# Stick-breaking attention: the later blocks' sum enters through a block's latest key, and two tokens of each block are swapped

## The chip, the cores and the metric

The kernel runs on one core of one Trainium2 chip. A core has a matrix engine (TensorE, PE in the profile; PEld is its loading of weights), VectorE (DVE), ScalarE (ACT), GpSimd (POOL) and SyncE (SP), which here issues the DMAs. The metric is the device time of one execution in microseconds, lower is better.

## The reference

The program is an encoder trunk of two layers over 1024 tokens of width 1024, each layer a mixer and a SwiGLU. The change is in layer 0's mixer, which has 8 heads of stick-breaking attention beside 8 heads of latent attention:

```
before = s_pos < t_pos
log_keep = jnp.where(before, jax.nn.log_sigmoid(-z), 0.0)
log_between = lax.cumsum(log_keep, axis=3, reverse=True) - log_keep
w_b = jnp.where(before, jnp.exp(jax.nn.log_sigmoid(z) + log_between), 0.0)
```

For a query t, each key s before it gets the weight of its own score times what all keys between s and t leave over. So the sum of `log_keep` runs over the keys from the latest one down to s, across all blocks of keys.

## The kernel before, in words

Keys stand in the 128 partitions, queries in the free dimension, two heads at a time (a pair, `p` = 0 to 3). A pass over one half of the queries (`hf`, 512 columns) goes through the blocks of 128 keys from the latest to the earliest, 4 blocks for the first half and 8 for the second, 48 block steps in all. Where a key block lies in the half itself (a diagonal step) only the later columns are worked on, 128, 256, 384 or 512 wide; the other steps have the full 512.

`sb_step` writes a block step as three stages. `scores` makes the scores z in a pair of PSUM banks (L894, L895), clips them into SBUF (L897, VectorE), takes exp and ln of 1 + exp (L898, L899, ScalarE), takes the larger of that and the score (L900, VectorE), clears the entries above the diagonal with a select on POOL (L888), and splits the result t into a rounded part sh (L904, ScalarE) and a rest sl (through the helper's line L248: head 0 on VectorE, head 1 on POOL). `weights` sums over keys with matrix products: a triangular matrix of ones, `tri`, times sh (L916) and times sl (L921), and for all blocks but the first a matrix of ones times `carry` (L919). The carry is a tile whose rows 0 and 32 hold the rounded part (L923, ScalarE) and the rest (L924, VectorE) of the row 0 of the sum, which is the sum over all keys so far. Then come the subtraction z minus sum (L927), exp (L928) and for diagonal steps the select again. `outputs` multiplies the weights with the values, one head per product (L831).

`step` keeps the stages of several blocks in flight. With LAG = 2, a block's `weights` are written two steps after its `scores`, and its `outputs` two after that. Between the steps `weave` puts filling work, projections for the next pair (L280 to L282) or, in pair 3, the preparation of the latent attention; `cost` and `total` set how much. A scheduler then orders the instructions of each engine, except in the feed-forward parts, which are pinned. An engine runs its instructions in that order. Tile tags bound how far ahead things may go: two pairs of score banks (`z`), three tiles `b` (t and the carry), four tiles `c` (sh and sl).

Of the kernel before, what the change touches and what calls it, by code (L numbers as in the profile page):

```python
# [22 lines left out]

GROUPS = [3, 3, 3, 2]
NEG = -(2.0 ** 100)
ZMAX = 88.0
MM_US = 0.216
HEAP = 60
# [2 lines left out]
LAG = 2  # L31
# [125 lines left out]
class Trunk:  # L157
# [47 lines left out]
    def load_consts(self):  # L205
        nc, a, cp = self.nc, self.a, self.cp
        self.g = cp.tile([P, G_N], F32, name="gains")
        nc.sync.dma_start(self.g, a["gains"])
# [8 lines left out]
        nc.gpsimd.affine_select(out=raw[:, 0:P], in_=self.ones, pattern=[[-1, P]], compare_op=ALU.is_ge,  # L217
                                fill=0.0, base=0, channel_multiplier=1)
        nc.vector.memset(raw[:, P:2 * P], 1.0)
        nc.vector.memset(raw[:, 2 * P:], 0.0)  # L220
        self.masks = cp.tile([P, HALF], F32R, name="masks")
        nc.vector.tensor_copy(self.masks, raw)
        self.tri, self.carry_ones = self.masks[:, 0:P], self.masks[:, P:2 * P]
        self.zeros = self.masks[:, 2 * P:3 * P]
# [650 lines left out]
    def sb_step(self, p, hf, j, proj, vt, st, o_d):  # L875
        nc = self.nc
        mm = nc.tensor.matmul
# [4 lines left out]
        top = j == 4 * hf + 3  # L882
        c0 = r * P if diag else 0
        cs = slice(c0, HALF)
        x = {}

        def causal(t):
            nc.gpsimd.affine_select(out=t, in_=t, pattern=[[0, 2], [1, P]], compare_op=ALU.is_gt,  # L888
                                    fill=0.0, base=0, channel_multiplier=-1)

        def scores():
            z = self.banks()
# [7 lines left out]
            nc.vector.tensor_tensor(t[:, :, cs], t[:, :, cs], zc[:, :, cs], ALU.max)  # L900
# [3 lines left out]
            nc.scalar.copy(sh[:, :, cs], t[:, :, cs])  # L904
            for e in range(2):
                self.rest(("dve", "pool")[e], sl[:, e, cs], t[:, e, cs], sh[:, e, cs])
            x.update(zc=zc, sh=sh, sl=sl)

        def weights():
            if top:  # L910
                st["carry"] = self.tmp("b", F32R)
                nc.gpsimd.memset(st["carry"].bitcast(F32), 0.0)
            carry = st["carry"]
            b = self.banks()
            for e in range(2):
                mm(b[:, e, cs], self.tri, x["sh"][:, e, cs], start=True, stop=False)  # L916
            if not top:
                for e in range(2):
                    mm(b[:, e, cs], self.carry_ones, carry[:, e, cs], start=False, stop=False)  # L919
            for e in range(2):  # L920
                mm(b[:, e, cs], self.tri, x["sl"][:, e, cs], start=False, stop=True)  # L921
            if j > 0:
                nc.scalar.copy(carry[0:1, :, cs], b[0:1, :, cs])  # L923
                nc.vector.tensor_tensor(carry[32:33, :, cs], b[0:1, :, cs], carry[0:1, :, cs].bitcast(F32),  # L924
                                        ALU.subtract)
            w = x["zc"]
            nc.vector.tensor_tensor(w[:, :, cs], w[:, :, cs], b[:, :, cs], ALU.subtract)  # L927
            nc.scalar.activation(w[:, :, cs], w[:, :, cs], AF.Exp)  # L928
            if diag:
                causal(w[:, :, c0:c0 + P])  # L930
# [469 lines left out]
    return np.stack([_ktiles(w, np.arange(i, i + m)) for i in range(0, w.shape[1], m)])  # L1400


def _layout(i):
    out = {}
    xT = np.ascontiguousarray(i["x"][0].T)
# [46 lines left out]
    s = np.arange(P)[:, None]  # L1452
    x = np.arange(640)[None, :]
    out["bias_k"] = np.ascontiguousarray(rb[:, np.clip(x - s, -256, 256) + 256])
    out["bias_q"] = np.ascontiguousarray(rb[:, np.clip(512 + s - x, -256, 256) + 256])
    pos = np.arange(S, dtype=np.float32)
# [32 lines left out]
```

## Time and profile before

| what | us |
|---|---|
| median of three runs (lowest, highest) | 2609.49 (2604.78, 2610.32) |
| the profiled execution's own time | 2615.43 |
| its span, first to last instruction | 2613.3 |
| PE busy in the span | 2521.6 |
| VectorE busy | 1911.5 |
| ScalarE busy | 1169.0 |
| POOL busy | 522.9 |

Busy time of a matrix product includes its way through the array; products follow each other at less than their own duration. A row of a group gives line, engine, operation, output<-input by name, shape and count, then busy us and the mean ns of one, then the idle us of the engine just before them and what ended it. A row in order of time gives start and duration in us.

### The profile page before, as it was taken

The numbers are of one execution on the slowest core, as the hardware profiler recorded it, in microseconds if no ns is written. First come the engines' busy times: TensorE is split into PE (matmuls) and PEld (weight loads), VectorE is DVE, ScalarE is ACT, GpSimd is POOL, SyncE is SP. The second block draws the span as 40 slices with busy tenths as digits, with TensorE's granted clock in tenths as the row PEclk, the third lists the DMA queues.
The fourth block names the chain that finished last, engine by engine and source line by source line (L and its number), as shares of the span: only waits on it lengthen the run. The fifth ranks groups of instructions, "written<-read, shape, count | busy, mean of one in ns | idle before, by whom it ended". The sixth has DMA issues, their size and how long they took to land.

```text
span 2613.3 us, 33627 instructions
## 1 busy us (share of the span) xinstructions
PE 2521.6 (96%) x11758; PEld 1941.0 (74%) x11758; DVE 1911.5 (73%) x3072; ACT 1169.0 (45%) x2028; POOL 522.9 (20%) x489
## 2 busy tenths in 40 slices
PE   7999999999999999999999999999999999999997
PEld 6766765557778888888787666676777888888876
DVE  6888887775787666777666777777778766667776
ACT  4677676454454334432253333334444443443324
POOL 3333324663000000000021333335400000000004
PEclk9999998999999999999999999999999999999999
DMA  4221100125434344476642222222552434447661
GB/s 137 61 63 53 53 17 29 35 64 159 163 99 161 110 140 142 149 258 216 206 160 67 73 78 80 73 69 89 172 166 96 162 109 141 145 140 260 213 213 69
DMA packets 179433, 319.70 MB, mean 122 GB/s; under 512 B 20545, under 2 KB 36801, under 8 KB 179265
## 3 DMA queue, kind: packets, MB, share of 16 engines
q1 hardware_dynamic: 179264, 317.56, 36.8%
q8 instruction: 93, 1.52, 0.3%
q14 instruction: 76, 0.61, 0.1%
HBM read 222.58 MB, written 84.41 MB: 117 GB/s over the span
## 4 chain that ended last, share of the span: by engine, by line
PE 68%; DVE 12%; DMA 2%; issue 2%; ACT 2%; SPq 0%; DVEq 0%; ACTq 0%
PE z L74 24%; PE mm L74 12%; PE o L74 6%; PE mm L280 5%; PE mm L281 5%; PE mm L282 5%; PE o L831 3%; DVE u L74 2%; DVE f L1093 2%; PE z L1201 1%; PE z L1175 1%; PE z L1202 1%; DVE u L303 1%; DMA wr<-in_w_down 1%; PE z L1088 1%
## 5 line engine op out<-in xcount | busy, mean ns | idle before, releaser
L74 PE MATMUL z<-u,vh 128*128 128x512 f32 x976 | 304.6, 393 | 7.2 <-DVE u L74 7.2
L74 PE MATMUL z<-u,wh 128*128 128x512 f32 x976 | 302.3, 390 | 6.5 <-DVE u L74 6.5
L280 PE MATMUL mm<-u,wh 128*128 128x512 f32 x720 | 291.7, 405 | 2.4 <-DVE u L710 1.1
L281 PE MATMUL mm<-u,wh 128*128 128x512 f32 x720 | 284.4, 395 | 1.4 <-DVE u L248 1.4
L248 POOL TENSOR_TENSOR wl<-wr,wh 128x512 fp32r<-128x512 f32 (+2 forms) x95 | 123.6, 1308 | 802.4 <-ACT wh L243 733.6
L282 PE MATMUL mm<-u,wl 128*128 128x512 f32 x720 | 283.8, 394 | 0.0
L74 PE MATMUL mm<-u,wh 128*128 128x512 f32 x720 | 224.6, 393 | 3.8 <-ACT wh L74 3.8
L74 PEld LDWEIGHTS z<-u,vh 128*128 128x128 f32 x976 | 184.5, 189 | 48.1 <-ACT u L74 8.8
L74 PEld LDWEIGHTS z<-u,wh 128*128 128x128 f32 x976 | 183.1, 188 | 47.4 <-DVE u L74 9.4
L74 PE MATMUL z<-u,vl 128*128 128x512 f32 x488 | 191.1, 392 | 0.0
L74 PE MATMUL z<-u,wl 128*128 128x512 f32 x488 | 190.0, 389 | 0.0
L280 PEld LDWEIGHTS mm<-u,wh 128*128 128x128 f32 x720 | 135.6, 188 | 62.2 <-issue 33.1
L831 PE MATMUL o<-a,u 128*64 128x512 f32 (+3 forms) x768 | 172.4, 485 | 0.3 <-ACT a L1204 0.3
L74 PEld LDWEIGHTS mm<-u,wh 128*128 128x128 f32 x720 | 135.5, 189 | 34.9 <-ACT wh L74 5.7
L281 PEld LDWEIGHTS mm<-u,wh 128*128 128x128 f32 x720 | 135.8, 189 | 32.5 <-issue 8.3
L282 PEld LDWEIGHTS mm<-u,wl 128*128 128x128 f32 x720 | 135.5, 188 | 32.3 <-issue 3.6
L74 PE MATMUL mm<-u,vh 128*128 128x512 f32 x496 | 152.7, 389 | 0.0
L248 POOL TENSOR_TENSOR u<-wr,u 128x512 fp32r<-128x512 f32 x8 | 10.9, 1373 | 671.7 <-ACT u L243 671.7
L74 PE MATMUL mm<-u,wl 128*128 128x512 f32 x360 | 141.2, 392 | 0.7 <-DVE wl L74 0.5
L1204 ACT ACTIVATE a<-a 128x1024 f32<-128x1024 f32 (+3 forms) x96 | 70.6, 738 | 155.3 <-DVE a L1203 155.0
L1072 POOL TENSOR_TENSOR b<-b,a 128x512 f32<-128x512 f32 (+3 forms) x80 | 110.6, 1382 | 135.8 <-ACT a L1204 117.4
L1203 DVE TENSOR_TENSOR a<-z,bias 128x1024 f32<-128x1024 f32 (+3 forms) x96 | 78.7, 823 | 79.5 <-PE z L1202 65.6
(248 smaller groups left out, 5983.1 us busy)
## 6 DMA issues: line engine op xcount, KB each, us to landing
u<-f_t SPq DMA_DIRECT2D x144, 256.0 KB, 5.2
vr<-in_w_up SPq DMA_DIRECT2D x88, 256.0 KB, 4.4
wr<-in_w_gate SPq DMA_DIRECT2D x88, 256.0 KB, 3.5
f_t<-x SPq DMA_DIRECT2D x72, 256.0 KB, 2.0
wr<-in_w_out SPq DMA_DIRECT2D x64, 256.0 KB, 3.0
f_t<-e SPq DMA_DIRECT2D x54, 256.0 KB, 3.6
ld<-f SPq DMA_DIRECT2D x54, 256.0 KB, 5.2
h<-u SPq DMA_DIRECT2D x48, 256.0 KB, 2.5
```

The lines of the kernel that those rows point to most:

```text
L74: return lambda *a, **k: self.tc.keep_in_program_order(f(*a, **k))
L248: self.eng(eng).tensor_tensor(lo, src, hi.bitcast(F32), ALU.subtract)
L280: mm(out, wh, xh, start=first, stop=False, skip_group_check=onto)
L281: mm(out, wh, xl, start=False, stop=False, skip_group_check=onto)
L282: mm(out, wl, xh, start=False, stop=last, skip_group_check=onto)
L303: self.eng(eng).tensor_tensor(acc, acc, sq, ALU.add)
L831: self.nc.tensor.matmul(o[rh, cs], vt[j // 4][:, j % 4, rh], w[:, e, cs], start=first, stop=last)
L1072: self.eng("dve" if dest[2] else "pool").tensor_tensor(st["esum"][:, :, cs], old[:, :, cs], ex[:, :, cs], ALU.add)
L1088: nc.tensor.matmul(den[64 * e:64 * e + 64, :], self.ones[:, 0:64], esum[:, e, :], start=True, stop=True)
L1093: nc.vector.scalar_tensor_tensor(r, t, 2.0, r, ALU.add, ALU.mult)
L1203: nc.vector.tensor_tensor(ex[:, :, cs], z[:, :, cs], tk[:, :, xs], ALU.add)
L1204: nc.scalar.activation(ex[:, :, cs], ex[:, :, cs], AF.Exp)
```

## The change

The rows of `order` shown here use names with a serial number (z_1225 is a pair of banks, here the sum of one block; b_ is t, c_ is sh or sl, a_ the clipped score and later the weight, mm_ and wh_ / wl_ belong to filling projections, o_ is the output).

A block step gets a stage `parts` between `scores` and `weights`. It adds row 0 of the later block's sum, from PSUM, to one row of t, and only then splits t into sh and sl. Since `tri` sums from the latest key down, a value added at the block's latest key reaches all keys of the block, and row 0 of the new sum again holds everything so far. The products with the matrix of ones, the carry tile with its cast, its subtraction and its clearing are gone.

[...] The triangular order is no longer that of the partitions; a 128 x 128 matrix `before` is loaded, `tri` is ones minus that matrix, and the two diagonal masks are multiplications with it on POOL instead of selects. Lines of the changed kernel: minimum L898, exp and ln L899 and L900, maximum L901, mask L890, row addition L910, cast L912, rests L250, sums L921, subtraction L924, exp L925, outputs L833.

```
 def causal(t):
-    nc.gpsimd.affine_select(out=t, in_=t, pattern=[[0, 2], [1, P]], compare_op=ALU.is_gt,
-                            fill=0.0, base=0, channel_multiplier=-1)
+    nc.gpsimd.tensor_tensor(t, t, self.before[:, None, :].to_broadcast([P, 2, P]), ALU.mult)
...
+    x.update(zc=zc, t=t)
+
+def parts():
+    t = x["t"]
+    if not top:
+        above, c1 = st["sum"]
+        nc.vector.tensor_tensor(t[LATEST:LATEST + 1, :, c1:], t[LATEST:LATEST + 1, :, c1:], above[0:1, :, c1:], ALU.add)
     sh, sl = self.tmp("c", F32R), self.tmp("c", F32R)
     nc.scalar.copy(sh[:, :, cs], t[:, :, cs])
...
 def weights():
-    if top:
-        st["carry"] = self.tmp("b", F32R)
-        nc.gpsimd.memset(st["carry"].bitcast(F32), 0.0)
-    carry = st["carry"]
     b = self.banks()
-    for e in range(2):
-        mm(b[:, e, cs], self.tri, x["sh"][:, e, cs], start=True, stop=False)
-    if not top:
+    for part in ("sh", "sl"):
         for e in range(2):
-            mm(b[:, e, cs], self.carry_ones, carry[:, e, cs], start=False, stop=False)
-    for e in range(2):
-        mm(b[:, e, cs], self.tri, x["sl"][:, e, cs], start=False, stop=True)
-    if j > 0:
-        nc.scalar.copy(carry[0:1, :, cs], b[0:1, :, cs])
-        nc.vector.tensor_tensor(carry[32:33, :, cs], b[0:1, :, cs], carry[0:1, :, cs].bitcast(F32),
-                                ALU.subtract)
+            mm(b[:, e, cs], self.tri, x[part][:, e, cs], start=part == "sh", stop=part == "sl")
+    st["sum"] = b, c0
...
-idle = [lambda: None] * (LAG - 1)
-self.step(scores, *idle, weights, *idle, outputs)
+idle = lambda: None
+self.step(scores, parts, weights, idle, outputs)
...
+order = np.arange(P)
+order[[LATEST, P - 1]] = order[[P - 1, LATEST]]
...
+self.before = cp.tile([P, P], F32, name="before")
+nc.sync.dma_start(self.before, a["before"])
 raw = self.tmp("f")
...
+nc.vector.tensor_tensor(raw[:, 0:P], self.ones, self.before, ALU.subtract)
+nc.vector.memset(raw[:, P:], 0.0)
```

The order on VectorE in the full-width steps of pair 0, second half. Before (L924 makes the carry's rest from the sum z_1252, L927 is the subtraction of the same sum):

```order
L924 TENSOR_TENSOR b_999<-z_1252,b_999 1x1024
L248 TENSOR_TENSOR c_1177<-b_1171,c_1176 128x512
L927 TENSOR_TENSOR a_1125<-a_1125,z_1252 128x1024
L897 TENSOR_SCALAR a_1268<-z_1263 128x1024
L897 TENSOR_SCALAR a_1334<-z_1329 128x1024
L924 TENSOR_TENSOR b_999<-z_1318,b_999 1x1024
L900 TENSOR_TENSOR b_1269<-b_1269,a_1268 128x1024
L927 TENSOR_TENSOR a_1170<-a_1170,z_1318 128x1024
```

The same place in the changed kernel (L924 is now the subtraction, L910 the row addition of the same sum; L250 to c_ is the rest of head 0):

```order
L924 TENSOR_TENSOR a_1106<-a_1106,z_1225 128x1024
L901 TENSOR_TENSOR b_1149<-b_1149,a_1148 128x1024
L898 TENSOR_SCALAR a_1243<-z_1238 128x1024
L910 TENSOR_TENSOR b_1149<-b_1149,z_1225 1x1024
L247 CAST wh_1381<-wr_1379 128x512
L250 TENSOR_TENSOR wl_1382<-wr_1379,wh_1381 128x512
L250 TENSOR_TENSOR c_1234<-b_1149,c_1233 128x512
L901 TENSOR_TENSOR b_1244<-b_1244,a_1243 128x1024
L924 TENSOR_TENSOR a_1148<-a_1148,z_1288 128x1024
L910 TENSOR_TENSOR b_1244<-b_1244,z_1288 1x1024
```

Where the row for the carry stood ahead of the subtraction and the rest c_ did not need it, the subtraction now stands first, the row addition behind it, and the rest c_1234 behind the row addition of z_1225.

The order on PE in the same steps. Before (one block's sum z_1387 in a row: tri times sh, ones times carry, tri times sl):

```order
L831 MATMUL o_1104<-a_1125,u_526 64x512 x2
L916 MATMUL z_1387<-c_1274,masks 128x512 x2
L919 MATMUL z_1387<-b_999,masks 128x512 x2
L921 MATMUL z_1387<-c_1275,masks 128x512 x2
L894 MATMUL z_1398<-u_873,u_1082 128x128
L895 MATMUL z_1398<-u_873,u_1084 128x128
```

In the changed kernel (z_1354 is the sum of the same block):

```order
L283 MATMUL mm_1391<-u_207,wh_1381 128x512
L284 MATMUL mm_1391<-u_206,wl_1382 128x512
L833 MATMUL o_1083<-a_1148,u_527 64x512
L921 MATMUL z_1354<-c_1296,masks 128x512 x2
L921 MATMUL z_1354<-c_1297,masks 128x512 x2
L895 MATMUL z_1367<-u_863,u_1061 128x128
L896 MATMUL z_1367<-u_863,u_1063 128x128
L895 MATMUL z_1367<-u_864,u_1062 128x128
L896 MATMUL z_1367<-u_864,u_1064 128x128
L833 MATMUL o_1083<-a_1148,u_527 64x512
```

The products with the carry are gone from the sum, and the two heads of one output (o_1083<-a_1148) stand on both sides of it.

More of the change, by code (lines that the diff above doesn't have):

```diff
@@ L25 @@
 NEG = -(2.0 ** 100)
+LATEST = 96
 ZMAX = 88.0
@@ L215, in load_consts @@
                                 fill=0.0, base=0, channel_multiplier=-1)
+        self.before = cp.tile([P, P], F32, name="before")
+        nc.sync.dma_start(self.before, a["before"])
         raw = self.tmp("f")
[L217 to L220, printed above, removed]
+        nc.vector.tensor_tensor(raw[:, 0:P], self.ones, self.before, ALU.subtract)
+        nc.vector.memset(raw[:, P:], 0.0)
         self.masks = cp.tile([P, HALF], F32R, name="masks")
         nc.vector.tensor_copy(self.masks, raw)
-        self.tri, self.carry_ones = self.masks[:, 0:P], self.masks[:, P:2 * P]
-        self.zeros = self.masks[:, 2 * P:3 * P]
+        self.tri, self.zeros = self.masks[:, 0:P], self.masks[:, P:2 * P]
         self.negblk = cp.tile([4, 4], F32, name="negblk")
@@ L906, in scores @@
                 self.rest(("dve", "pool")[e], sl[:, e, cs], t[:, e, cs], sh[:, e, cs])
[L907 removed]
+            x.update(sh=sh, sl=sl)
         def weights():
[L910 to L913 removed]
             b = self.banks()
[L915 to L917 removed]
+            for part in ("sh", "sl"):
                 for e in range(2):
[L919 to L925 removed]
+                    mm(b[:, e, cs], self.tri, x[part][:, e, cs], start=part == "sh", stop=part == "sl")
+            st["sum"] = b, c0
             w = x["zc"]
@@ L1400, in _mtiles, with _order @@
     return np.stack([_ktiles(w, np.arange(i, i + m)) for i in range(0, w.shape[1], m)])
+def _order():
+    order = np.arange(P)
+    order[[LATEST, P - 1]] = order[[P - 1, LATEST]]
+    return order
 def _layout(i):
     out = {}
-    xT = np.ascontiguousarray(i["x"][0].T)
+    perm = _order()
+    tokens = (np.arange(0, S, P)[:, None] + perm).reshape(-1)
+    out["before"] = (perm[:, None] < perm[None, :]).astype(np.float32)
+    xT = np.ascontiguousarray(i["x"][0][tokens].T)
     out["x"] = np.ascontiguousarray(xT.reshape(KD, P, 2, HALF).transpose(2, 0, 1, 3))
@@ L1451, in _layout @@
     rb = i["od_rel_bias"][0]
-    s = np.arange(P)[:, None]
-    x = np.arange(640)[None, :]
+    s = perm[:, None]
+    x = (np.arange(0, 640, P)[:, None] + perm).reshape(1, -1)
     out["bias_k"] = np.ascontiguousarray(rb[:, np.clip(x - s, -256, 256) + 256])
     out["bias_q"] = np.ascontiguousarray(rb[:, np.clip(512 + s - x, -256, 256) + 256])
-    pos = np.arange(S, dtype=np.float32)
+    pos = tokens.astype(np.float32)
     inv = (np.float32(10000.0) ** (-np.arange(0, 32, 2, dtype=np.float32) / np.float32(32))).astype(np.float32)
@@ L1487 @@
     y = r.results[0]["out_y"]
-    return np.ascontiguousarray(y.transpose(0, 3, 1, 2).reshape(1, S, D))
+    y = y.transpose(0, 3, 1, 2).reshape(S // P, P, D)
+    return np.ascontiguousarray(y[:, np.argsort(_order())].reshape(1, S, D))
```

## The prediction

> **What bounds the kernel now.** I read the page first, then the stages of the stick-breaking part, then the groups by line and shape, then single rows in order of time.
>
> ```profile
> span 2613.3 us, 33627 instructions
> PE 2521.6 (96%) x11758; PEld 1941.0 (74%) x11758; DVE 1911.5 (73%) x3072; ACT 1169.0 (45%) x2028; POOL 522.9 (20%) x489
> ```
>
> TensorE (PE) is busy for 96% of the span, so a product taken away is worth its time wherever PE stays the bound. The part that changes runs from about 60 to 420 us. Busy time per stage there, columns PE, PEld, DVE, ACT, POOL, granted clock:
>
> ```profile
> 109.00:147.00 38.00, 36.73 (x196) 26.57 (x195) 34.76 (x39) 27.75 (x38) 11.38 (x11) 1.00 0.15 41
> 183.00:220.00 37.00, 35.94 (x192) 26.25 (x192) 34.64 (x38) 26.43 (x36) 10.31 (x11) 1.00 0.16 47
> 256.00:294.00 38.00, 36.88 (x156) 24.96 (x155) 37.15 (x41) 26.88 (x32) 13.19 (x12) 1.00 0.21 57
> 360.00:400.00 40.00, 33.17 (x122) 20.96 (x120) 39.38 (x49) 27.64 (x43) 13.61 (x10) 0.87 0.05 15
> ```
>
> The first three rows are the full-width steps of pairs 0, 1 and 2: PE is the bound there, but VectorE (DVE) stands at 91, 94 and 98%. The last row lies in pair 3: VectorE has no pause and PE is idle for 6.8 of 40 us, so there VectorE sets the time.
>
> **What is removed.** 80 products of the carry with the ones matrix (L919), 40 casts (L923), 40 one-row subtractions (L924) and 8 clearings.
>
> ```profile
> L919 PE MATMUL z<-b,masks x80: 274/393/496, 82.0 to 416.2; 128*128 128x512 f32 x48, 128*128 128x256 f32 x16, 128*128 128x384 f32 x16
> 182.13 0.39 PE L894 MATMUL z<-u,u 128*128 128x512 f32 x1
> 182.36 0.39 PE L895 MATMUL z<-u,u 128*128 128x512 f32 x1
> 191.07 0.28 PE L281 MATMUL mm<-wl,u 128*128 128x256 f32 x1
> 191.19 0.28 PE L282 MATMUL mm<-wh,u 128*128 128x256 f32 x1
> ```
>
> Products overlap, so their price is the distance of their starts: 0.227 us at 512 columns (0.23 in this pair of rows), 0.12 at 256, by interpolation 0.17 at 384. 48 x 0.227 + 16 x 0.17 + 16 x 0.12 = **15.5 us of PE**. In pair 3 four of these steps lie in the stretch that VectorE sets; 8 x 0.227 = **1.8 us** of it is lost.
>
> ```profile
> L923 ACT CAST b<-z 1x1024 fp32r<-1x1024 f32 (+3 forms) x40 | 29.6, 741 | 13.4 <-PE z L921 13.2
> L924 DVE TENSOR_TENSOR b<-z,b 1x1024 fp32r<-1x1024 f32 x16 | 19.4, 1214 | 3.5 <-ACT b L923 3.0
> L912 POOL MEMSET b<- 128x1024 f32 x8 | 7.7, 957 | 0.0
> ```
>
> ScalarE is relieved of 29.6 us and POOL of 7.7 us; neither engine is a bound (45% and 20% of the span), so both count as nothing. The 40 subtractions are replaced by 40 row additions with the same shapes, one operand in PSUM and one in SBUF as before: VectorE's load stays the same. I take 1.21 us for one at 1024, by L924.
>
> **What is moved: the chain from block to block.** Before, the split into high and low parts didn't need the later block's sum; only L919 did, between the high and the low products. Now it runs: low products end, subtraction (L924 of the changed kernel), row addition, cast, rest on POOL, next low products. Durations:
>
> ```profile
> L927 DVE TENSOR_TENSOR a<-a,z 128x1024 f32<-128x1024 f32 x24 | 29.2, 1216 | 2.4 <-PE z L921 2.2
> L897 DVE TENSOR_SCALAR a<-z 128x1024 f32<-128x1024 f32 x24 | 29.2, 1216 | 5.0 <-PE z L895 4.8
> L904 ACT CAST c<-b 128x1024 fp32r<-128x1024 f32 x24 | 25.0, 1043 | 7.6 <-POOL b L888 6.5 <-DVE b L900 1.1
> 194.30 1.30 POOL L248 TENSOR_TENSOR c<-b,c 128x512 fp32r<-128x512 f32 x1 [5.77 <-issue]
> 196.07 1.21 DVE L900 TENSOR_TENSOR b<-b,a 128x1024 f32<-128x1024 f32 x1
> 127.79 1.08 PE L831 MATMUL o<-a,u 128*64 128x512 f32 x4
> 140.71 1.07 PE L831 MATMUL o<-a,u 128*64 128x512 f32 x2
> 141.71 0.50 PE L282 MATMUL mm<-u,wl 128*128 128x512 f32 x1
> ```
>
> Where the addition stands right behind the subtraction, the low part is ready 1.22 + 1.21 + 1.04 + 1.30 + 0.2 for the hops = 5.0 us after the low products before it. Where the order has a maximum and a minimum between them (z_1225 in the rows shown), 2.4 us more: 7.4 us. Against that stands PE's work between the two, counted from the order. From z_1225 to z_1288: 47 products of 256 and 2 of 512 columns, 6.05 us, then the high products and three score products, 1.14: PE arrives at 7.2 us and waits about 0.3. From z_1288 to z_1354: 1 + 6 of 512, 11 of 256, an output pair at 1.0, a lone head's output at 1.0, high products 0.45: 5.35 us against 5.0, no wait. The same sum for the 30 passages of pairs 0 to 2 leaves ten of them short, by 0.03 to 1.56 us, **4.0 us** together. If VectorE comes to each subtraction late by 0.25 us, it is 7.5 us; by 0.5, 12.2; by 1.0, 24.4. Queued behind a late addition are the next minimum and the weights' rests, so what is late next is a score bank and the filling products. Walking VectorE's rows through z_1225 to z_1354 at the durations above I find it 0.1 to 0.25 us late, so I take **7.5 us**; ends for the range: 4.0 and 24.4.
>
> The waits before the low products that exist now belong to the old order, and the 7.5 us stand in their place:
>
> ```profile
> L921 PE MATMUL z<-c,masks 128*128 128x512 f32 x48 | 16.2, 412 | 2.0 <-DVE c L248 1.3 <-POOL c L248 0.7
> L921 PE MATMUL z<-c,masks 128*128 128x384 f32 x16 | 4.2, 342 | 0.8 <-DVE c L248 0.8
> L921 PE MATMUL z<-c,masks 128*128 128x128 f32 x16 | 3.6, 277 | 1.3 <-POOL c L248 1.3
> ```
>
> 2.0 + 0.8 + 1.3 = **4.1 us** come back.
>
> **What the new order costs elsewhere.** Two heads' outputs side by side take 1.0 us (x4 above), one head alone takes as long (140.71 to 141.71). In the stick-breaking part four head pairs stood apart (512, 512, 384, 512 columns, 1.0 or 0.75 us each), now six do (four of 512, one of 384, one of 256 at 0.5), 5.25 us against 3.75: **+1.5 us**. The new constant is a load between the gains and x:
>
> ```profile
> 0.81 0.39 SPq L208 DMA_DIRECT2D gains<-in_gains  x1
> 1.26 0.42 SPq L187 DMA_DIRECT2D ld<-in_x  x1
> ```
>
> SyncE's issues stand 0.45 us apart, x and all behind it come that much later: **+0.4 us**. The masks' difference and cast lie in VectorE's pause before x arrives. The swapped layout changes no instruction's shape: 0.
>
> **The masks on POOL.** 64 selects become multiplications with a loaded mask, not shown before at this form; the nearest rows are a select, and POOL's two-input rest of the same 256 elements:
>
> ```profile
> L888 POOL TENSOR_SCALAR_AFFINE_SELECT b<-b 128x256 f32<-128x256 f32 x32 | 14.4, 450 | 80.0 <-DVE b L900 74.4 <-PE mm L281 3.1 <-PE z L894 2.1
> 81.28 0.74 POOL L248 TENSOR_TENSOR c<-b,c 128x256 fp32r<-128x256 f32 x1 [0.74 <-ACT c L904]
> 136.77 1.79 POOL L248 TENSOR_TENSOR c<-b,c 128x512 fp32r<-128x512 f32 x1 [9.36 <-ACT c L904]
> 137.33 2.31 DVE L900 TENSOR_TENSOR b<-b,a 128x1024 f32<-128x1024 f32 x1
> ```
>
> Between 0.45 and 0.74 each, I take 0.74 (it too reads two tensors): 64 x 0.3 = 19 us more on an engine that is busy 20% of the time, and the mask is due one step before the addition. I cost it at 0; if its cover is gone, see the second rival. The last two rows show how: a VectorE maximum that met POOL's rest took 2.31 us, not 1.21. The Trainium skill, SBUF — State Buffer, section "SBUF: two separate sides", says why: the two engines share a port pair, whoever starts first holds it for the whole instruction, and VectorE is shut out when both its inputs lie in SBUF. The trace agrees (1.10 us longer). By that rule the row additions, with one input in PSUM, never wait, but maxima and rests do.
>
> **Sum**, against the profiled execution's 2615.4 us: -15.5 + 1.8 - 4.1 + 7.5 + 1.5 + 0.4 = -8.4, so 2607.0. That execution lies 5.9 above the median of the runs shown (2609.5); against the median the forecast is **2601 us**.
>
> **Rivals.**
>
> First, the chain is covered better than I sum: 29.6 us less on ScalarE lets its casts start at once, and VectorE no longer waits for L923. For it: L924 waited 3.0 us for L923 at full width alone. Against it: VectorE's 98%. Then only 4.0 us of waits, and pair 3 keeps its share: -15.5 - 4.1 + 4.0 + 1.9 = -13.7, 2596 us. Chance 0.17.
>
> Second, the mask multiplications hold up VectorE in the diagonal steps (the mechanism of the rows 136.77 and 137.33). Pairs 0 to 2 have 48 of them; if 4 in 10 meet a two-SBUF instruction and hold it 0.74 us, that is 14 us of VectorE, and with half of it reaching PE, 7 us: 2608, no change. Against it: VectorE has pauses in the diagonal stretches. Chance 0.18.
>
> Third, the other side: the chain decides each full-width step. Its place is VectorE's queue ahead of the row addition. At 1.0 us late per passage the waits are 24.4 us: -15.5 + 1.8 - 4.1 + 24.4 + 1.9 = +8.5, 2618. It turns to a loss from about 0.7 us late. For it: VectorE at 91 to 98%, each of its instructions 1.2 us long, so an arrival in the middle of one costs half of that. Against it: while PE waits, VectorE catches up. Chance 0.17.
>
> Fourth, the change doesn't reach the clock at all, because the gain of pairs 0 to 2 runs into the VectorE stretch of pair 3 and waits there: 2609. Against it: VectorE's load before 360 us leaves it room to come earlier too. Chance 0.06.
>
> **How the numbers follow.** Forecast 0.42 (2596 to 2605 in itself), rivals 0.17, 0.18, 0.17, 0.06. A measurement of this kernel can tell about 0.2%, 5.2 us, from no change. Faster: 0.34 of the forecast, the first rival 0.17, 0.01 of the fourth: 0.52. Same: 0.08 of the forecast, 0.15 of the second, 0.01 and 0.03 of the third and fourth: 0.27. Slower: 0.03, 0.16 and 0.02: 0.21. The range 2590 to 2614 takes in the first two rivals and goes halfway into the third.
>
> **What would show it.** Right: no products with the ones matrix; PE busy about 15 us less; waits of L921 for the rests and the casts of 5 to 10 us together; from the first to the last tri product some 8 us less. Wrong: VectorE's maxima above 1.4 us in the mean (second rival); L921 waits above 15 us, with VectorE at 95% or more in the diagonals too (third); PE idle in pair 3 grown by what the earlier pairs gained (fourth).

## The result, and the profile after

| kernel | median us (lowest, highest; runs) | ratio to before, 95% interval |
|---|---|---|
| before | 2608.55 (2604.51, 2610.34; 6) | 1 |
| changed | 2623.30 (2615.97, 2626.08; 6) | 1.0056 [1.0041, 1.0072] |

The change makes the kernel slower by 14.6 us (0.0056 x 2608). The forecast was 2601 us, 8.4 us faster. Its range ended at 2614, so the sign and the range were both wrong. Among the experiments below, one run of e3 took 6586.76 us, far outside its other nine (2605 to 2612), and is left out.

The first two lines of the page of the changed kernel:

```profile
span 2620.6 us, 33417 instructions
...
PE 2511.9 (96%) x11678; PEld 1926.4 (74%) x11678; DVE 1933.0 (74%) x3072; ACT 1141.9 (44%) x1988; POOL 535.6 (20%) x480
```

The 80 products are gone (x11758 to x11678), ScalarE has 27 us less to do, and VectorE has 21.5 us *more*, at the same number of instructions. That growth is the first thing to explain, since the additions have the duration of the subtractions that they replace.

The profiled executions are 2622.66 us after and 2615.43 before, only 7.2 apart. To see where the difference lies I take the first dense product of the feed-forward part, which comes after everything that was changed. These are the views by source line of before and of the changed kernel (durations, then first and last start):

```profile
L74 PEld LDWEIGHTS mm<-u,wh x720: 186/188/331, 659.0 to 2539.1; 128*128 128x128 f32 x180
```

```profile
L76 PEld LDWEIGHTS mm<-u,wh x720: 186/188/329, 669.9 to 2546.5; 128*128 128x128 f32 x180
```

It starts 10.9 us later. From there to the end the profiled execution of before takes 3.6 us longer than that of the changed kernel, in work whose instructions the diff leaves as they were. That execution lies 6.9 us above its median, so the difference of the two profiles understates the loss.

Busy time per stage in the changed kernel, columns PE, PEld, DVE, ACT, POOL, granted clock:

```profile
60.00:160.00 100.00, 94.01 (x470) 67.88 (x471) 88.25 (x109) 56.49 (x89) 35.57 (x39) 1.00 0.22 61
160.00:260.00 100.00, 88.20 (x419) 59.93 (x419) 90.44 (x105) 59.20 (x87) 43.84 (x45) 0.97 0.19 55
260.00:360.00 100.00, 92.72 (x410) 65.42 (x409) 86.69 (x99) 55.95 (x76) 36.46 (x38) 1.00 0.17 48
360.00:440.00 80.00, 69.13 (x262) 44.76 (x260) 69.50 (x86) 53.87 (x99) 27.05 (x22) 0.94 0.07 21
```

and the same stages of before:

```profile
60.00:160.00 100.00, 96.33 (x491) 71.22 (x489) 84.80 (x113) 65.90 (x104) 33.44 (x44) 1.00 0.22 60
160.00:260.00 100.00, 96.31 (x484) 68.88 (x485) 87.59 (x111) 71.09 (x104) 40.17 (x53) 1.00 0.22 61
260.00:360.00 100.00, 98.86 (x445) 71.89 (x445) 82.55 (x104) 65.69 (x91) 32.62 (x39) 1.00 0.15 46
360.00:440.00 80.00, 69.07 (x263) 45.65 (x262) 69.44 (x85) 56.34 (x103) 30.08 (x23) 0.89 0.07 22
```

In pairs 0 to 2 (60 to 360 us) PE is idle for 25.1 us, against 8.5 before. In the last row, pair 3, PE's busy time is the same; the pair itself, from its first score product to its last triangular one, takes 131.4 us against 132.0. From the first triangular product of all to the last the changed kernel takes 351.3 us, 13.3 longer than before. The waits of PE from 40 to 440 us in the changed kernel (total, times, longest) say on what:

```profile
PE z L921 <- DVE c L250: 13.6, 21, 1.2
PE o L833 <- POOL a L890: 8.2, 8, 4.9
...
PE z L921 <- POOL c L250: 2.3, 4, 0.6
PE z L921 <- ACT c L912: 2.1, 4, 0.9
```

Before, the first and the third of these were:

```profile
PE z L921 <- DVE c L248: 2.0, 4, 0.8
PE z L921 <- POOL c L248: 2.0, 4, 1.1
```

So the triangular products wait 18.0 us for what comes out of the new chain, priced at 7.5, and the output products wait 8.2 us for a masked weight, priced at nothing. The groups by line and shape, 60 to 440 us, of the changed kernel (busy us, mean ns, idle before):

```profile
L250 POOL TENSOR_TENSOR c<-b,c 128x512 fp32r<-128x512 f32 x24 | 38.3, 1594 | 67.3 <-ACT c L912 65.2 <-POOL u L859 1.9
L250 DVE TENSOR_TENSOR c<-b,c 128x512 fp32r<-128x512 f32 x24 | 37.7, 1572 | 5.4 <-ACT c L912 4.9
...
L901 DVE TENSOR_TENSOR b<-b,a 128x1024 f32<-128x1024 f32 x24 | 30.7, 1279 | 0.2
...
L890 POOL TENSOR_TENSOR b<-b,before 128x256 f32<-128x256 f32 x32 | 28.4, 889 | 44.1 <-DVE b L901 29.6 <-issue 14.5
...
L910 DVE TENSOR_TENSOR b<-b,z 1x1024 f32<-1x1024 f32 x16 | 19.4, 1215 | 0.5
```

and of the rests and the maxima before:

```profile
L248 POOL TENSOR_TENSOR c<-b,c 128x512 fp32r<-128x512 f32 x24 | 35.3, 1470 | 80.0 <-ACT c L904 62.6 <-issue 17.3
...
L900 DVE TENSOR_TENSOR b<-b,a 128x1024 f32<-128x1024 f32 x24 | 31.5, 1313 | 2.6 <-ACT b L899 2.2
...
L248 DVE TENSOR_TENSOR c<-b,c 128x512 fp32r<-128x512 f32 x24 | 24.5, 1020 | 3.3 <-ACT c L904 3.2
```

The addition costs what was forecast (1215 ns), and the maxima have not grown (1279 ns; 1313 before). VectorE's rest has, from 1020 to 1572 ns: 13.2 us of VectorE's new load is in this one row. One passage shows how (start, duration; the rows are from the views of ScalarE, POOL, VectorE and PE in turn):

```profile
191.75 1.06 ACT L912 CAST c<-b 128x1024 fp32r<-128x1024 f32 x1
...
192.94 1.74 POOL L250 TENSOR_TENSOR c<-b,c 128x512 fp32r<-128x512 f32 x1 [0.41 <-POOL u L859]
...
192.84 0.68 DVE L250 TENSOR_TENSOR u<-u,u 64x512 fp32r<-64x512 f32 x1
193.44 1.79 DVE L250 TENSOR_TENSOR c<-b,c 128x512 fp32r<-128x512 f32 x1
...
195.28 0.74 PE L921 MATMUL z<-c,masks 128*128 128x512 f32 x2 [0.34 <-DVE c L250]
```

Both rests need the one cast, which ends at 192.81. POOL's starts first, since VectorE has another piece of 0.68 us ahead of its own, and VectorE's lasts until 0.55 us after POOL's has ended (195.23 against 194.68). The low products start 2.47 us after the cast; the forecast gave this link 1.30 us and a hop. Over the 19 full-width passages from 60 to 360 us, the mean from the cast's end to the end of the later rest is 2.35 us. It was 1.93 us before already (21 passages), only not on a chain from block to block.

### The profile page after: what moved, and what is told of

It is laid out like the page before. It is cut to its first block, busy times and chain, and to the rows that moved or that the text cites. A ratio compares the mean times of both kernels' runs of the same rounds, so it can differ in the third digit from the quotient of the medians.

```text
span 2620.6 us, 33417 instructions
## 1 busy us (share of the span) xinstructions
PE 2511.9 (96%) x11678; PEld 1926.4 (74%) x11678; DVE 1933.0 (74%) x3072; ACT 1141.9 (44%) x1988; POOL 535.6 (20%) x480
## 4 chain that ended last, share of the span: by engine, by line
PE 72%; DVE 18%; issue 3%; ACT 3%; DMA 3%; POOL 1%; SPq 0%; DVEq 0%; POOLq 0%; ACTq 0%
PE z L76 24%; PE mm L76 12%; PE o L76 6%; PE mm L282 6%; PE mm L283 6%; PE mm L284 6%; PE o L833 4%; DVE u L76 2%; DVE f L1090 2%; PE z L1198 1%; DVE c L250 1%; PE z L1172 1%; DVE wl L250 1%; DVE b L901 1%; PE z L1199 1%
## 5 line engine op out<-in xcount | busy, mean ns | idle before, releaser
L250 POOL TENSOR_TENSOR wl<-wr,wh 128x512 fp32r<-128x512 f32 (+2 forms) x95 | 125.0, 1322 | 792.3 <-ACT wh L245 723.6
L833 PE MATMUL o<-a,u 128*64 128x512 f32 (+3 forms) x768 | 174.8, 486 | 9.3 <-POOL a L890 8.2
L250 POOL TENSOR_TENSOR u<-wr,u 128x512 fp32r<-128x512 f32 x8 | 10.9, 1375 | 669.3 <-ACT u L245 669.3
```

Source lines behind the costliest of these rows:

```text
L250: self.eng(eng).tensor_tensor(lo, src, hi.bitcast(F32), ALU.subtract)
L833: self.nc.tensor.matmul(o[rh, cs], vt[j // 4][:, j % 4, rh], w[:, e, cs], start=first, stop=last)
```

## Experiments

In each run a scheduler orders the instructions anew, so an edit may move a few hundred rows besides its own. Times in us below are (ratio - 1) x 2608, and the uncertainty of a difference of two is worked out from both intervals.

| edit | median us (runs) | ratio, 95% interval | us to before |
|---|---|---|---|
| changed kernel | 2623.30 (6) | 1.0056 [1.0041, 1.0072] | +14.6 |
| e1: before, masks multiplied | 2612.18 (10) | 1.0015 [1.0006, 1.0024] | +3.9 |
| e2: changed, old selects | 2617.60 (8) | 1.0033 [1.0023, 1.0044] | +8.6 |
| e3: changed, sum not handed on | 2609.33 (9) | 1.0004 [0.9994, 1.0014] | +1.0 |
| e5: changed, addition first | 2622.23 (4) | 1.0053 [1.0038, 1.0068] | +13.8 |
| e4: changed, both rests on VectorE | 2612.27 (10) | 1.0014 [1.0005, 1.0024] | +3.7 |
| e6: changed, copy on ScalarE | 2611.59 (10) | 1.0010 [0.9999, 1.0021] | +2.6 |
| e7: before, copy on ScalarE | 2598.93 (8) | 0.9963 [0.9953, 0.9973] | -9.6 |
| e8: e6, addition first | 2600.68 (8) | 0.9972 [0.9961, 0.9982] | -7.3 |
| e9: before, both rests on VectorE | 2601.30 (5) | 0.9968 [0.9956, 0.9981] | -8.3 |
| e11: before, both edits | 2598.16 (5) | 0.9951 [0.9937, 0.9965] | -12.8 |
| e12: changed, both edits | 2595.29 (5) | 0.9948 [0.9935, 0.9960] | -13.6 |
| e10: e12, addition first | 2591.45 (5) | 0.9933 [0.9921, 0.9946] | -17.5 |
| e13: changed, row added to itself | 2615.08 (5) | 1.0034 [1.0021, 1.0046] | +8.9 |
| e14: e13, old selects | 2607.05 (11) | 0.9994 [0.9985, 1.0004] | -1.6 |
| e15: e4, old selects | 2610.34 (11) | 1.0006 [0.9997, 1.0015] | +1.6 |
| e16: e4, addition first | 2615.99 (5) | 1.0035 [1.0022, 1.0047] | +9.1 |
| e17: e13, copy on ScalarE | 2613.44 (12) | 1.0017 [1.0008, 1.0027] | +4.4 |
| e18: e14, copy on ScalarE | 2605.39 (12) | 0.9985 [0.9974, 0.9995] | -3.9 |

My theory at the start was that the chain from block to block is longer than priced (the rests) and that the masks cost something. The rivals were VectorE's fullness, and the masks alone.

### The masks: e1 and e2

```
 e1, in before:
-    nc.gpsimd.affine_select(out=t, in_=t, pattern=[[0, 2], [1, P]], ...)
+    nc.gpsimd.tensor_tensor(t, t, self.before[:, None, :].to_broadcast([P, 2, P]), ALU.mult)
 e2, in the changed kernel: the same the other way round
```

> The kernel before, with the loaded mask and the 64 multiplications on POOL in place of the selects, and nothing else: no swap of tokens, the carry as it was. My theory now is that the change lost in two places, the masks (8.2 us of PE waiting for POOL's masks ahead of the outputs in the changed kernel's profile) and the chain through the row addition (18.0 us of PE waiting ahead of the low products). By it the masks alone make the kernel before 4 to 10 us slower. Rival: the chain alone is the loss and the masks are hidden as predicted; then within 3 us of the kernel before.

> The changed kernel with the old selects in place of the multiplications. Left out: the selects follow the order of the partitions, so the two swapped tokens of each block are masked by their place and not by their time; every other instruction is that of the changed kernel. Theory of two places: 6 to 10 us faster than the changed kernel, so some 5 to 9 us slower than the kernel before. Rival, the chain alone: within 3 us of the changed kernel, 12 to 17 us slower than the kernel before.

The edit of e1 is shown without the lines that load the mask, so its figure includes that load. e2 masks the two swapped tokens of each block of 128 (96 and 127) by their place, not by their order. The multiplications cost 3.9 us (+-2.4) in the kernel before and 6.0 (+-4.9) in the changed kernel, each at the lower edge of what my theory said. The forecast had 0, with the price left to the second rival. But the row in which that rival should have shown itself, the maxima, has not grown. What the masks delay is their own readers. In e2 the waits of PE are:

```profile
PE z L922 <- DVE c L250: 14.1, 24, 1.2
PE o L833 <- POOL a L890: 5.2, 2, 4.6
```

The output products wait twice instead of eight times (the longest 4.6 us, close to the changed kernel's 4.9), and the waits for the rests are untouched. So the masks are one part of the loss, and by these two runs the smaller one.

### The sum that goes into the row: e3, e13

```
 e3:
-    nc.vector.tensor_tensor(t[LATEST:LATEST + 1, :, c1:], t[LATEST:LATEST + 1, :, c1:], above[0:1, :, c1:], ALU.add)
+    nc.vector.tensor_tensor(above[0:1, :, c1:], t[LATEST:LATEST + 1, :, c1:], above[0:1, :, c1:], ALU.add)
 e13:
+    nc.vector.tensor_tensor(t[LATEST:LATEST + 1, :, c1:], t[LATEST:LATEST + 1, :, c1:], t[LATEST:LATEST + 1, :, c1:], ALU.add)
```

> The changed kernel with the row addition written back into the bank that it reads, so that the split no longer waits for it. Left out: the later blocks' sum doesn't reach the block; VectorE does the same number of additions of the same shapes. Theory: 14 to 20 us of waits go, 2603 to 2609 us, about the kernel before or up to 5 us faster, with the masks' 8 us still in it. Rival, VectorE's load or the masks are the loss and not the order of the chain: within 5 us of the changed kernel.

> The changed kernel with the row of the latest key added to itself instead of to the later block's row: the addition stays on VectorE, in its place, but waits for no other block, and holds no bank of the earlier sums (the later blocks' sums are left out of the result). Chain theory (the length from block to block is what cost the changed kernel): the chain is gone altogether, so the gain of the products shows, less the masks' multiplications (some 6 us by the run with the old selects): 2598 to 2605. Rival (VectorE's fullness and the rests that hold each other up cost as much without any chain): 2608 to 2616.

In both the later blocks' sums are left out of the result. In e3 the addition stays on VectorE, reads the later block's sum and writes it back there, so the cast no longer waits for it. In e13 the addition still stands ahead of the cast in its own block, but waits for no other block. Its inputs then both lie in SBUF, where e3 has one in PSUM; it lasts as long in both, 1219 and 1222 ns at full width. e3 is at +1.0, at the upper edge of its range. e13 misses my theory's range (2598 to 2605) and falls into the rival's: without any link between blocks the kernel is still 8.9 us slower than before. The two together cut the loss up:

- from the changed kernel to e13, the link between blocks: 5.7 us (+-5.2), barely resolved;
- from e13 to e3, the addition ahead of the cast *inside* a block: 7.9 us (+-4.2), in spite of 3.5 us of a new wait in e3, for the bank that its addition writes.

So a theory of the chain between blocks alone falls. A block's own way from its scores to its low products has grown by an addition, and this by itself costs about as much.

### The order on VectorE: e5

```
 def parts():
     ... row addition ...
+    st["less"]()          # the subtraction, exp and mask of the block before
 def weights():
     ... sums ...
-    subtraction, exp, mask
+    st["less"] = lambda: less(b)      # for j == 0 at once
```

> The changed kernel with the row addition ahead of the subtraction of the same sum: the subtraction, its exp and its mask are written behind the next block's addition. Same instructions, the chain shorter by one subtraction of 1.21 us in most full-width steps. Theory, the length of the chain decides: 8 to 16 us faster than the changed kernel, so between 6 us faster and 7 us slower than the kernel before. Rival, the two rests that hold each other up on the shared port are all of the loss: the chain is shorter, but its end stays as it is, and most of 18 us stays: at most 4 us faster than the changed kernel.

No gain (13.8 against 14.6), where 8 to 16 us were expected. The subtraction of 1.2 us ahead of the addition is not what decides. The waits only change their names, 19.0 us together (18.0 in the changed kernel), among them a new one for the bank that the late subtraction holds:

```profile
PE z L922 <- DVE c L250: 8.5, 13, 1.6
...
PE z L922 <- DVE a L930: 4.1, 4, 1.8
```

### Rests and VectorE's fullness: e4, e6, e7, e8

```
 e4:
-    self.rest(("dve", "pool")[e], sl[:, e, cs], t[:, e, cs], sh[:, e, cs])
+    self.rest("dve", sl[:, e, cs], t[:, e, cs], sh[:, e, cs])
 e6 (changed kernel), e7 (before), e8 (e5 and e6):
-    nc.vector.tensor_scalar(zc[:, :, cs], z[:, :, cs], ZMAX, None, ALU.min)
+    nc.scalar.copy(zc[:, :, cs], z[:, :, cs])
```

> The changed kernel with both heads' rests on VectorE instead of one on POOL. In the changed kernel the VectorE rest takes 1.57 us at 512 columns (1.02 before): it starts with POOL's and they hold each other up. Port theory (the two rests side by side are the loss): 8 to 12 us faster than the changed kernel, since 0.72 + 0.72 us behind each other end sooner than 1.3 + 0.7. VectorE theory (VectorE bounds the full-width steps): what POOL hands over, some 28 us of work, is about what the held-up rests give back, within 5 us of the changed kernel.

> The changed kernel with the score's way out of PSUM on ScalarE (a copy) instead of VectorE (a minimum with 88). Left out: the clip at 88, which these scores don't reach. It takes 46 us of VectorE and gives some 42 us to ScalarE. The runs so far: without the chain the changed kernel only comes back to the time before, with 11 us less PE work and VectorE at 80 to 93%; with the addition first nothing is won. VectorE theory: the full-width steps are bounded by VectorE, so the products that went freed nothing there; with VectorE relieved 14 us or more go, 2600 to 2609 us. Chain theory (length of the chain decides): the chain isn't shorter by it, so at most 6 us faster than the changed kernel, 2617 or more.

> The same move in the kernel before: the score's copy on ScalarE, the clip left out. VectorE theory, if PE and VectorE bound the kernel before in turn: 0 to 6 us faster, since its PE waits in the stick-breaking part are only some 8 us. Then the difference between the changed kernel and this one, both with the move, is the change without VectorE's bound: the changed one is 3 to 10 us faster. Chain theory: the changed one stays 8 us or more slower than this one.

> Both: the row addition ahead of the subtraction, and the score's copy on ScalarE. VectorE theory: once VectorE is no longer the bound, the shorter chain counts: 3 to 8 us faster than the move alone. Rival: the subtraction put behind holds the next sum's bank (4.1 us of PE waiting for it in the run with the addition first), so within 3 us of the move alone.

e6, e7 and e8, and later e10, e11, e12, e17 and e18, leave out the clip of the score at 88.

e4 brings 10.9 us back (+-4.8), as the theory of the rests expected. A rest on VectorE then takes 738 ns in the mean, so two of them one after the other (1476 ns) are done sooner than the one that had shared the work with POOL (1572 ns). The group of e4:

```profile
L250 DVE TENSOR_TENSOR c<-b,c 128x512 fp32r<-128x512 f32 x48 | 33.6, 738 | 0.3
```

e6 brings 12.0 us back (+-5.0) by another way: VectorE gets 48 instructions less, of 1.2 us each at full width. Its time lies between the ranges of both theories. But the same edit in the kernel before brings 9.6, more than the 0 to 6 expected, so the change costs 12.2 us (+-3.9) also where VectorE has room. VectorE's fullness alone is not the cause either. With room there, the order matters: e8 is 9.9 us (+-4.0) under e6 (3 to 8 were expected), although the same reordering brought nothing in e5.

### The controls, and both cures at once: e9 to e12

```
 e9, e11: e4's edit in before, and in e7;  e12: e4's edit in e6;  e10: e4's edit in e8
```

> The kernel before, with both heads' rests on VectorE. Port theory (GpSimd's rest that starts first stops VectorE's for its whole length, and this costs the changed kernel because there it happens on nearly every step, 19 of 24 full-width ones against 8 of 24 before): here little is stopped, VectorE gains the work of a second rest (24 x 0.68 us less the 0.34 us that each of its own is now held up, some 8 to 13 us in all) and the time is the same or worse, 2608 to 2618. Rival (GpSimd's rests are simply slow, and both rests on VectorE are better anywhere): 2600 or less.

> The kernel before with the score's copy on ScalarE and both rests on VectorE, the counterpart without the change of the run with all three edits. Port theory: VectorE has room here, and few rests are held up, so 2597 to 2601, the same as with the copy alone (2599). Rival (GpSimd's rests are slow anywhere): 2595 or less.

> The changed kernel with the score's copy on ScalarE and both rests on VectorE, the addition where the change put it. Port theory: about 10 us under the same kernel with the rests split (2611.6), 2599 to 2604, since the waits on the rests (17 us in the four pairs there) mostly go. Rival (VectorE's fullness is what the split hurt, already cured by the copy's move): 2608 to 2612, no gain from a second cure.

> The changed kernel with the three relieving edits at once: the score's copy on ScalarE (no clip at 88), the row's addition issued ahead of the earlier block's subtraction, both rests on VectorE. Theory (the block to block chain takes the gain, by the held-up rests and by VectorE's fullness): with all three the PE waits on the rests go under 5 us in the four pairs and the gain of some 10 us of products shows against the kernel before with the same copy (2599): 2588 to 2594. Rival (the addition in a row costs PE something that no relief gives back, or the room gained is used up by VectorE's two rests): 2598 or more.

e9 corrects my theory. I expected no gain from it, since in the kernel before the rests are held up less often. It gains 8.3 us, which is close to what its rival said (2600 or less; 2601.30). So the split of the rests is a poor choice in *both* kernels, and with it undone in both the change still costs 12.0 us (+-4.1).

Only together do the two cures turn the result: e12 is level with e11 (1.2 us lower in the mean of five runs each on the same chip), and with the addition first, e10, the changed kernel is under both, by 3.9 us under e12 and by 5.0 under e11 in the means; its runs lie from 2590.36 to 2594.12, those of e11 from 2592.61 to 2599.47. e10 and e11 are where the theory had them (2588 to 2594, 2597 to 2601); e12 went below its range.

The waits of PE for the low products, 40 to 440 us, tell why one cure isn't enough. With the rests on VectorE alone (e4), VectorE is busy for 264.5 of 300 us, the addition comes late in its queue, and the products wait for the cast behind it. In the two longest waits, 2.3 us each, the cast then starts 0.8 us after the addition's end, behind an activation on ScalarE:

```profile
PE z L921 <- ACT c L912: 6.2, 4, 2.3
...
PE o L833 <- POOL a L890: 4.0, 6, 1.5
PE z L921 <- DVE c L250: 3.2, 6, 1.6
PE o L833 <- ACT a L925: 2.8, 2, 1.9
```

With the copy moved alone (e6) VectorE has room (233.3 of 300 us), but the rests still hold each other up:

```profile
PE z L921 <- DVE c L250: 11.9, 14, 1.0
...
PE z L921 <- POOL c L250: 2.7, 6, 0.6
```

With both (e12) little is left of either:

```profile
PE z L921 <- DVE c L250: 2.5, 3, 1.4
...
PE z L921 <- ACT c L912: 1.0, 1, 1.0
```

The busy times from 60 to 360 us of e4, e6 and e12 (PE, PEld, DVE, ACT, POOL):

```profile
60.00:360.00 300.00, 286.13 (x1331) 206.62 (x1332) 264.46 (x365) 179.37 (x259) 62.80 (x82) 0.97 0.20 55
```

```profile
60.00:360.00 300.00, 284.66 (x1341) 203.03 (x1343) 233.25 (x279) 208.77 (x307) 121.32 (x125) 0.99 0.19 55
```

```profile
60.00:360.00 300.00, 293.27 (x1401) 210.70 (x1400) 244.25 (x341) 218.76 (x320) 69.02 (x83) 1.00 0.20 56
```

PE is idle for 13.9, 15.3 and 6.7 us in them, 25.1 in the changed kernel, 8.5 before.

### What was left: e14 to e18

```
 e14, e15: e2's edit in e13, and in e4;  e16: e4's edit in e5;  e17, e18: e6's edit in e13, and in e14
```

> The same with the diagonal masks by the old select (the two swapped tokens are masked by place). If the masks' multiplications cost about 6 us whatever the chain is: 2592 to 2599, or 6 under the run with the row added to itself. If they cost only as a part of the chain from block to block: within 2 us of that run.

> The changed kernel with both rests on VectorE and the old selects (the two swapped tokens masked by place). The changed kernel with both rests on VectorE is 1.0014 of before, the kernel before with the same is 0.9968: 12 us apart, with 6.8 us of PE's waits for masked weights (o L833) and 9.4 for the rests. If the masks are half of it: 2604 to 2608. If the chain through a full VectorE is nearly all of it: 2609 to 2613.

> The changed kernel with both rests on VectorE and the row's addition issued ahead of the earlier block's subtraction, the score's copy left on VectorE. If what is left of the cost there is the place of the addition in VectorE's queue (the subtraction of 1.2 us ahead of it): 2600 to 2606. If it is VectorE's fullness, whatever the order: 2609 to 2613, as without the reordering (it gained nothing with the rests split).

> The changed kernel with the row of the latest key added to itself (no link from block to block; the later blocks' sums are left out) and the score's copy on ScalarE, which relieves VectorE (no clip at 88). It differs from the changed kernel with that copy (1.0010 of before) by the link between blocks alone, and from the run with the row added to itself (1.0034) by the copy alone. If the link costs its 10 us also where VectorE has room, because the rests hold each other up on it: 2598 to 2603. If without the link VectorE's fullness was what was left, nothing else: 2593 to 2598. If neither (the row's addition itself or the masks cost it): 2606 or more.

> The same with the old selects (the two swapped tokens masked by place). Here products are removed, no link, no masks' multiplications, VectorE relieved: if the sum of the parts is right, the gain of the products shows against the kernel before with the same copy (2599): 2586 to 2592. If the row's addition costs what the products brought: 2597 or more.

e14 and e18 leave out the later sums and mask the swapped tokens by place, e15 only the latter, e17 only the former.

- **Masks.** With POOL also doing a rest, the multiplications cost 10.5 us (e13 to e14, +-4.1; e14 was expected at 2592 to 2599 and is at 2607, since e13 was too high already) and 8.3 (e17 to e18, +-3.8); with the rests on VectorE 2.1 (e4 to e15, +-3.5), not to be told from nothing. So it is probably POOL's two jobs together that make them dear. That isn't quite shown: e13 and e17 have no link, e4 has one, and with the link in both kernels 6.0 and 2.1 can't be told apart. The masks aren't half of what e4 has left.
- **Order.** e16 is 5.5 us (+-4.1) *slower* than e4, outside both its ranges (2600 to 2606, 2609 to 2613). The subtraction that was put back holds its bank for longer: 2.8 us of PE's waits are for that bank, where e4 has none. But one wait of 3.8 us in the preparation of the latent attention (L1036) is new as well, and which of the two decides was not separated.
- **The link.** With the copy on ScalarE, taking the link away brings nothing: e17 is at +4.4, e6 at +2.6 (difference 1.8, +-3.9). Its expected 2598 to 2603 was missed by 10 us; the case of 2606 or more, the addition itself or the masks, is the one that came.
- **Products removed, nothing else in the way.** e18 should have shown the whole gain, 2586 to 2592. It is at -3.9, still 5.7 us (+-3.8) worse than the kernel before with the same copy. With the rests split, an addition ahead of the cast, together with the split's new place one stage later, costs more than the 80 products brought, with no link and no multiplication. Its waits:

```profile
PE z L922 <- DVE c L250: 5.9, 7, 1.3
...
PE z L922 <- POOL c L250: 3.1, 6, 0.6
```

## Why the prediction was wrong

**The step that failed is the sum for the moved chain: "1.22 + 1.21 + 1.04 + 1.30 + 0.2 for the hops = 5.0 us".** Its first three terms hold: 1215 ns for the subtraction, 1215 for the addition, 1.05 us for the cast; so do the hops, 0.24 us from addition to cast in the mean of 30 passages of pairs 0 to 2. The rest was mis-sized: it was taken from one row of POOL's rest alone (1.30), with VectorE's beside it. It is 2.35 us until both rests are there, 1.0 us more. The prediction even had a price for a passage that is late by 1.0 us: 24.4 us of waits, and a time of 2618. Measured were 18.0 us of waits, where its list has some 0.7 us of lateness and a time of about 2612. So the lateness that it put in, 0.25 us, was wrong, because lateness was looked for in VectorE's queue *ahead* of the addition only; and the list alone doesn't reach the measured 2623. The rows that showed the step stood in the prediction: a rest of POOL of 1.79 us, and a maximum of 2.31 us that had met it. They were used for the masks and not for the rests, though the mean of POOL's rest was 1470 ns before already. (A slip beside it changes nothing: 7.4 us against 7.2 leaves a wait of 0.2, not 0.3.)

**The chain was drawn between blocks only.** The runs put 7.9 us on the addition ahead of the cast within a block (e13 to e3) and 5.7 on the link, the latter barely resolved and gone when VectorE has room (e17). The prediction compared the chain with the PE work from one block's low products to the next one's. A block's own way from its maximum to its low products, which became longer by the addition, was not summed at all.

**"I cost it at 0"** for the masks: 3.9 to 10.5 us with POOL's rests beside them, 2.1 without. POOL's 20% is a mean over the span. In 60 to 360 us it is 116 of 300, and its instructions there stand close together, a rest that is held up next to a mask. As an estimate, the two terms, 18.0 - 7.5 for the chain and 8.2 for the masks, put 18.7 us on the forecast of 2601, 2620; some 4 us stay open.

**What held.** The products' number and the addition's 1.21 us. Pair 3 neither gained nor lost, and the pairs before it gained nothing that could have waited there, so the fourth rival is out. Of the signs for being right only the missing products came: PE's busy time fell by 9.7 us, not 15, and the way from the first triangular product to the last grew by 13.3 us, where it should have shrunk by 8. The second rival's mechanism is real but struck the rests, not the maxima, which stayed at 1.28 us. The third rival came nearest, with both its signs: L921 waits above 15 us, and VectorE at 96 and 97% in two stretches with diagonal steps of the changed kernel:

```profile
80.00:100.00 20.00, 18.75 (x89) 12.68 (x87) 19.18 (x26) 13.61 (x21) 10.20 (x13) 1.00 0.25 65
...
140.00:160.00 20.00, 18.90 (x83) 11.99 (x82) 19.39 (x25) 10.52 (x17) 7.34 (x8) 1.00 0.25 73
```

Its place was wrong, though: with the addition put first (e5) nothing was gained.

**What stays open.** e10 shows a gain of some 5 us over e11, not the 12 that remain of the 15.5 us of products after the prediction's small terms. Where the rest went wasn't tried (one piece shows: PE waits 5.2 us for L992 in e10, in the preparation of the latent attention, and 2.4 us for the same work in e11); e10's masks are multiplications still, and the split heads' outputs (1.5 us by the forecast) were not measured alone. The change also moved the split of t from a block's first stage to its second, and no run moved it alone: its part of the cost isn't known. Nor was the row added to itself run with both rests on VectorE, which would price the addition inside the block without the held-up rests. The three shares of the loss (link, addition ahead of the cast, masks) don't add up by themselves, since each depends on what else is late.

## What to carry to other kernels

An operation that is put ahead of a cast or a split lengthens every block's own way as well as any link between blocks. Sum both, up to the *last* of the pieces that the next product needs. Where two engines share one job, look in the trace for both pieces released together before taking the duration of one that ran alone. And when one cure brings nothing, or as much in the kernel before, try the cures together and in both kernels: here each alone left the change 12 us behind, and both with the new order put it in front.

## What the runs showed of the hardware

A rest of 128x512 with both inputs in SBUF takes VectorE 0.69 us where POOL's doesn't come before it, and POOL 1.29 us alone. Where both are due at once they run one after the other, whoever is first. The two orders, from the changed kernel in order of time, VectorE's rest each time, the first with the row ahead of it:

```profile
131.37 0.69 DVE L250 TENSOR_TENSOR wl<-wr,wh 128x512 fp32r<-128x512 f32 x1
131.98 1.77 DVE L250 TENSOR_TENSOR c<-b,c 128x512 fp32r<-128x512 f32 x1
...
393.90 0.69 DVE L250 TENSOR_TENSOR c<-b,c 128x512 fp32r<-128x512 f32 x1
```

and POOL's:

```profile
131.45 1.76 POOL L250 TENSOR_TENSOR c<-b,c 128x512 fp32r<-128x512 f32 x1 [7.29 <-ACT c L912]
...
393.95 1.79 POOL L250 TENSOR_TENSOR c<-b,c 128x512 fp32r<-128x512 f32 x1 [1.97 <-ACT c L912]
```

In the earlier pair POOL is first by 0.53 us, and VectorE's rest ends 0.54 us after POOL's; POOL's is itself longer than 1.29, since a rest of weights on VectorE (wl) had begun 0.08 us before it. In the later pair VectorE is first by 0.05, and POOL's takes 1.79. In the changed kernel 21 of the 24 full-width rests of VectorE took over 1.1 us, before 7 of 24. The Trainium skill, SBUF — State Buffer, section "SBUF: two separate sides", says that VectorE with two SBUF inputs and GpSimd share a port pair, and that whichever starts first has it for the whole instruction. These rows agree; I had cited the sentence and priced it for the masks' rival only. So splitting this job over the two engines saves nothing when one cast releases both. The masks meet VectorE's instructions with two inputs in SBUF in the same way, maxima and rests of weights above all: 20 of the 64 took over 0.85 us, each while such an instruction, begun before it, was running. The view by source line of the changed kernel (shortest, median, longest ns) has the forecast's 0.74 us as the median, and a tail that makes the mean 889 ns:

```profile
L890 POOL TENSOR_TENSOR b<-b,before x32: 722/744/1230, 75.3 to 355.1; 128x256 f32<-128x256 f32 x32
```
